# Second mixture of experts: whole experts, tiles of whole weight rows, and another sharing of the low parts between two engines

## The chip, the core and the metric

The kernel runs on one core of one Trainium2 chip. The core has five engines that run side by side and wait for each other through semaphores: PE (TensorE, matrix products, with its weight load PEld), DVE (VectorE), ACT (ScalarE), POOL (GpSimd) and SP (SyncE, which here only issues transfers). Each engine takes its instructions strictly in the order of its own queue. SBUF is the memory beside the engines, PSUM the small memory into which PE accumulates; 16 DMA engines move data between HBM and SBUF.

The metric is the time of the whole program on the device, in microseconds (us). Lower is better.

## The reference, cut to what matters

The program computes two transformer-like blocks one after the other. The change touches only the last stage: the second mixture of experts, in which each of 16 experts picks its own 128 tokens out of 1024.

```python
D_MODEL = 1024; SEQ = 1024; N_EXPERTS_2 = 16; CAPACITY_FACTOR = 2; D_EXPERT_2 = 1024

def expert_choice_ffn(h, w_router, w_gate, w_up, w_down):
    B, S, D = h.shape
    cap = CAPACITY_FACTOR * S // N_EXPERTS_2                      # 128 tokens for each expert
    aff = jax.nn.softmax((h @ w_router).astype(jnp.float32), axis=-1)
    gates, idx = lax.top_k(aff.transpose(0, 2, 1), cap)
    bidx = jnp.arange(B)[:, None, None]
    xe = h[bidx, idx]
    hg = jnp.einsum('becd,edf->becf', xe, w_gate)                 # 128 x 1024 x 1024 per expert
    hu = jnp.einsum('becd,edf->becf', xe, w_up)
    y = jnp.einsum('becf,efd->becd', jax.nn.silu(hg) * hu, w_down)
    y = y * gates[..., None].astype(y.dtype)
    return jnp.zeros_like(h).at[bidx, idx].add(y)

# in second_block: h2 = rmsnorm(x, norm2_w) * (1 + sc2) + sh2;  x = x + gt2 * expert_choice_ffn(h2, ...)
```

All is in float32. The weights of this stage are 16 x 3 matrices of 1024 x 1024, 4 MB each.

## The kernel before

The stage is the class `Moe2`; its `run` (from line 2466) is what the change rewrites, with `load` (line 2335), which issues the weight loads, and the lists made in `open`.

**Three products for one.** PE gets float32 precision out of two parts of each operand. `split_hi_lo` (lines 51 to 61) makes the high part on ACT (a copy that rounds, line 55, tile `wh`) and the low part as the difference of the value and its high part on DVE or, if told so, on POOL (line 61, tile `wl`). `mm3` (lines 64 to 67) then issues three matmuls of 128 x 512: high with high (line 65), high with low (line 66), low with high (line 67). Each reads 128 tokens' activations as the stationary side and 512 columns of weights as the moving side.

**Units and tiles.** An expert is cut in two units of 512 hidden columns (`units`, 32 of them). A unit has six weight tiles of 1 MB, each four blocks of 128 rows by 512 columns: two of gate, two of up, two of down. So a row of a tile is 512 floats out of a matrix row of 1024. The tiles sit in 13 buffers (pools of `WA` = 6 and `WB` = 7), taken in turn; `load(n)` issues the next n transfers on SP's queue in the order of `order`, and a transfer waits until the last reader of its buffer is done.

**Chunks.** `split(u, i)` makes of each product (i = 0 gate, 1 up, 2 down) four chunks of 128 x 1024 floats: one ACT operation for `wh`, one DVE or POOL operation for `wl`; both come from rings of seven buffers (pool `d_s`). A chunk feeds six matmuls, so an expert has 24 chunks and 144 matmuls. POOL makes the low part where `u == 0` (all twelve chunks of the first unit) and for `PL = (1, 0)`: the first two chunks of up, one right behind the other, in each unit, four for an expert. All other low parts are DVE's.

**Order.** The program's order is `gate_up(u)`, then (after an expert's first unit) `gather(e + 1)` and `choose(e + 3)`, then `down(u - 1)`, so that the product of one unit covers the step from `h` to `hh` of the unit before. `gate_up` accumulates in PSUM buffers `pg` and `pu`, `h` is silu(gate) by ACT times up by DVE, one buffer of 512 columns. `down` transposes `h` on PE (tile `tp`), splits it in `hh` and `hl` (one buffer each), and accumulates in `py0` and `py1` over both units of an expert; after the second unit DVE scales the result into `y` (line 2565) and POOL adds it to the output with an indirect DMA (line 2567). `gather` fetches an expert's 128 rows with an indirect DMA of POOL into `xg` (two buffers), scales, transposes and splits them into `xh` and `xl`; `choose` makes the list of rows from one-hot tiles `oh` (DVE, line 2487) and small matmuls (line 2491). A planner that works at build time gives each engine's queue its order from the program's order and modelled times, so neighbouring steps are interleaved on each engine.

Of the kernel before, what the change touches and what calls it, by code (L numbers as in the profile page):

```python
# [9 lines left out]
FR = mybir.dt.float32r  # L10
BF = mybir.dt.bfloat16
# [32 lines left out]
def bcast(ap, shape):  # L44
    return ap.to_broadcast(shape)
# [792 lines left out]
def ind(ap):  # L838
    return bass.IndirectOffsetOnAxis(ap=ap, axis=0)
# [1433 lines left out]

NX = 16
CAP = 128
PL = (1, 0)
XR = D + 1 + NX
WA = 6
WB = 7
# [2 lines left out]
class Moe2:  # L2282
# [3 lines left out]
    def open(self):  # L2286
        k, ident = self.k, self.ident
        nc, tc, T, sb = k.nc, k.tc, k.T, k.sb
        V, PE = nc.vector, nc.tensor
        self.es = ExitStack()  # L2290
        self.ps_s = ExitStack()
        cp = self.cp = self.es.enter_context(tc.tile_pool(name="d_c", bufs=1, reuse_waits="tile"))
        pp = self.pp = self.ps_s.enter_context(
            tc.tile_pool(name="d_rp", bufs=1, space=PSUM, side="right", reuse_waits="tile"))
        self.t_s = ExitStack()
        tp = self.tp = self.t_s.enter_context(tc.tile_pool(name="d_t", bufs=1, side="right", reuse_waits="tile"))
        wr = sb(tp, [P, 8, NX], tag="wr")
# [16 lines left out]
        self.units = [(e, hf) for e in range(NX) for hf in range(2)]  # L2314
        self.order = [(0, i) for i in range(4)]
        for u in range(len(self.units)):
            self.order += [(u + 1, i) for i in range(4) if u + 1 < len(self.units)] + [(u, 4), (u, 5)]
# [18 lines left out]
    def load(self, n):  # L2336
        k = self.k
        for _ in range(n):
            if self.next == len(self.order):
                return  # L2340
            u, i = self.order[self.next]
            e, hf = self.units[u]
# [3 lines left out]
            if i < 4:  # L2346
                src = k.T[("w_gate_2", "w_up_2")[i // 2]][0, e][512 * (i % 2):512 * (i % 2) + 512,
                                                                512 * hf:512 * hf + 512]
            else:
                src = k.T["w_down_2"][0, e][512 * hf:512 * hf + 512, 512 * (i - 4):512 * (i - 4) + 512]  # L2350
            k.nc.sync.dma_start(out=t, in_=src.rearrange("(k p) n -> p k n", p=P))

    def each(self, xc, i, q):
# [112 lines left out]
    def run(self):  # L2466
# [5 lines left out]
        units, wt, load = self.units, self.wt, self.load  # L2472
        slots = WA + WB
        xt, hs, ys = {}, {}, {}
# [6 lines left out]
        with tc.tile_pool(name="d_k", bufs=2, side="right", reuse_waits="tile") as wk, \  # L2481
                tc.tile_pool(name="d_p", bufs=1, space=PSUM, reuse_waits="tile") as pp:

            def choose(e):
                oh = sb(wk, [P, 2, 4, P], BF, tag="oh", bufs=1)
                for h in range(2):
                    V.tensor_tensor(oh[:, h], bcast(self.pos[:, h, :, e:e + 1], [P, 4, P]),
                                    bcast(self.slot.unsqueeze(1), [P, 4, P]), op=OP.is_equal)
                ps = sb(pp, [P, 4, P], tag="tp", bufs=2)[:, 0, 0:2]
                for i in range(NT):  # L2490
                    PE.matmul(ps, oh[:, i // 4, i % 4], self.tk[:, i % 4 * 2 + i // 4], start=i == 0, stop=i == NT - 1)
                V.tensor_scalar(self.idx[:, e:e + 1], ps[:, 0:1], ps[:, 1:2], None, op0=OP.add)

            def gather(e):
                xg = sb(wk, [P, XR], tag="xg")
                dma = G.indirect_dma_start(out=xg, out_offset=None, in_=self.x4_d, in_offset=ind(self.idx[:, e:e + 1]))
                xh = sb(wk, [P, 8, P], FR, tag="xh")
                xl = sb(wk, [P, 8, P], FR, tag="xl")
# [19 lines left out]
                    split_hi_lo(k, xh[:, ks], xl[:, ks], t)  # L2518
                return dma.ins

            def split(u, i):
                r = []
                for c in range(4):
                    wh = sb(wp, [P, 2, 512], FR, tag="wh")
                    wl = sb(wp, [P, 2, 512], FR, tag="wl")
                    src = wt[u, 2 * i + c // 2][:, c % 2 * 2:c % 2 * 2 + 2]
                    split_hi_lo(k, wh, wl, src, lo_eng="pool" if u == 0 or (i, c // 2) == PL else "dve")
                    r.append((wh, wl))
                return r

            def gate_up(u):
                e, hf = units[u]
                xh, xl = xt[e]
                pg = sb(pp, [P, 512], tag="pg", bufs=2)
                pu = sb(pp, [P, 512], tag="pu", bufs=2)
                for i, ps in ((0, pg), (1, pu)):
                    ws = split(u, i)
                    for kk in range(8):
                        wh, wl = ws[kk // 2]
                        mm3(nc, ps, xh[:, kk, :], xl[:, kk, :], wh[:, kk % 2, :], wl[:, kk % 2, :], kk == 0, kk == 7)  # L2540
                h = sb(wk, [P, 512], tag="h", bufs=1)
                A.activation(h, pg, AF.Silu)
                V.tensor_tensor(h, pu, h, op=OP.mult)
                hs[u] = h

            def down(u):
                e, hf = units[u]
                ps = sb(pp, [P, 4, P], tag="tp", bufs=2)
                for j in range(4):
                    PE.transpose(ps[:, j, :], hs[u][:, j * P:(j + 1) * P], ident)  # L2550
                hh = sb(wk, [P, 4, P], FR, tag="hh", bufs=1)
                hl = sb(wk, [P, 4, P], FR, tag="hl", bufs=1)
                split_hi_lo(k, hh, hl, ps)
                if hf == 0:
                    ys[e] = [sb(pp, [P, 512], tag=f"py{n}") for n in range(2)]
                ws = split(u, 2)
                for n in range(2):
                    for j in range(4):
                        wh, wl = ws[2 * n + j // 2]
                        mm3(nc, ys[e][n], hh[:, j, :], hl[:, j, :], wh[:, j % 2, :], wl[:, j % 2, :],  # L2560
                            hf == 0 and j == 0, hf == 1 and j == 3)
                if hf == 1:
                    y = sb(wk, [P, D], tag="y", bufs=1)
                    for n in range(2):
                        V.scalar_tensor_tensor(y[:, 512 * n:512 * n + 512], ys[e][n], self.gcol[:, e:e + 1],
                                               gt2[:, 512 * n:512 * n + 512], op0=OP.mult, op1=OP.mult)
                    G.indirect_dma_start(out=self.out, out_offset=ind(self.idx[:, e:e + 1]), in_=y, in_offset=None,
                                         compute_op=OP.add)
# [6 lines left out]
            for u in range(len(units)):  # L2575
                e, hf = units[u]
                with tc.issue_after(self.exp) if u == 0 else ExitStack():
                    gate_up(u)
                load(4)
                if hf == 0 and e + 1 < NX:  # L2580
                    gather(e + 1)
                    if e + 3 < NX:
                        choose(e + 3)
                if u:
                    down(u - 1)
                    load(2)
            down(len(units) - 1)
        self.es.close()


# [61 lines left out]
```

## Time and profile before

| | |
|---|---|
| median of 3 runs | 3712.46 us (3711.19 to 3718.37) |
| the profiled execution: its time | 3718.16 us |
| the profiled execution: its span, first to last instruction | 3716.4 us |
| busy share of the span | PE 90%, DVE 54%, ACT 35%, POOL 31% |
| mean granted clock of TensorE | 0.959 of full |
| transferred | 856.7 MB, 231 GB/s over the span |

The profile is one execution. An engine's busy time counts its instructions from start to end, and neighbouring ones overlap a little. A wait is put down to what ended it. The stage of the change begins at about 3042 us of the span (routing, with the first low parts beside it), its first large matmul starts at 3083 us, and its last result is added to the output at the end of the span.

### The profile page before, as it was taken

To read this page: it belongs to the slowest core of one execution; us is meant where nothing else is said; L and a number is where in the kernel's file an instruction comes from. 1 tells how busy PE (TensorE), PEld (TensorE's weight loads), DVE (VectorE), ACT (ScalarE), POOL (GpSimd) and SP (SyncE) were. 2 spreads that over 40 slices of the span, in tenths; PEclk is the share of its full clock that TensorE was granted. 3 is DMA by queue.
4 is the path that set the end of the run, shared out by engine and by line. 5 is a ranking of instruction groups with operands and counts; after the bars stand their busy time and mean duration, and the time that the engine had idled before them with its cause. 6 is when DMAs were issued, how large, how long until landed. Compare 5 with 4: busy or idle time off the path is not lost. (4 is left out here: it accounts for less than half of the span.)

```text
span 3716.4 us, 58458 instructions
## 1 busy us (share of the span) xinstructions
PE 3354.9 (90%) x23203; PEld 2589.5 (70%) x23203; DVE 2002.5 (54%) x3563; ACT 1287.1 (35%) x2200; POOL 1164.0 (31%) x1139
## 2 busy tenths in 40 slices
PE   6887899989999999999769988889999977999998
PEld 5676777976676666665368766676777975777776
DVE  7676765252222111211056776735676447999887
ACT  4321132310000000000043333326554236888776
POOL 3477632311001111111122334333232234545343
PEclk9998999999999999999979999999999988999999
DMA  8721224269989999999843234452225556999995
GB/s 239 225 77 52 62 100 153 84 237 383 389 330 398 399 394 397 393 400 408 329 131 99 71 108 117 126 159 86 78 77 141 199 175 248 352 364 366 354 328 191
DMA packets 479317, 856.70 MB, mean 231 GB/s; under 512 B 100779, under 2 KB 294075, under 8 KB 428608
## 3 DMA queue, kind: packets, MB, share of 16 engines
q1 hardware_dynamic: 440288, 786.04, 58.5%
q0 software_dynamic: 16464, 36.39, 4.1%
q10 hardware_dynamic: 22288, 30.48, 2.5%
q8 instruction: 185, 3.03, 0.3%
q14 instruction: 92, 0.75, 0.1%
HBM read 770.37 MB, written 90.74 MB: 232 GB/s over the span
## 5 line engine op out<-in xcount | busy, mean ns | idle before, releaser
L1109 PE MATMUL gu<-w,xt 128*64 128x256 f32 x4096 | 486.4, 385 | 10.5 <-DMA w<-in_expert_w_gate 9.2
L61 DVE TENSOR_TENSOR wl<-w,wh 128x1024 fp32r<-128x1024 f32 x310 | 454.7, 1513 | 45.8 <-ACT wh L55 45.0
L55 ACT ACTIVATE wh<-w 128x1024 fp32r<-128x1024 f32 x412 | 419.7, 1058 | 118.5 <-PE pg L67 32.4
L1109 PEld LDWEIGHTS gu<-w,xt 128*64 128x64 f32 x4096 | 285.2, 137 | 175.5 <-issue 26.1
L1098 POOL DMA_INDIRECT x2d<-ys,si x64 | 114.7, 1792 | 909.8 <-ACT ys L1133 856.2
L61 POOL TENSOR_TENSOR wl<-w,wh 128x1024 fp32r<-128x1024 f32 x102 | 289.3, 2851 | 276.3 <-ACT wh L55 221.2
L1193 PE MATMUL xg<-oh,xh 128*128 128x256 f32 x1024 | 262.1, 293 | 7.1 <-DVE xt L1211 7.1
L1121 ACT ACTIVATE h<-gu 128x256 f32<-128x256 f32 x64 | 24.6, 384 | 673.4 <-PE gu L1109 666.1
L1193 PE MATMUL xg<-oh,xl 128*128 128x256 f32 x1024 | 253.5, 285 | 0.0
L1130 PE MATMUL y<-w,hts 128*64 128x512 f32 x1024 | 235.3, 599 | 1.4 <-ACT ys L1133 1.1
L1193 PEld LDWEIGHTS xg<-oh,xh 128*128 128x128 f32 x1024 | 193.0, 189 | 51.0 <-issue 34.3
L1211 DVE SCALAR_TENSOR_TENSOR xt<-xg,gcolp,row 128x256 f32<-128x256 f32 x128 | 60.3, 481 | 277.2 <-PE xg L1193 216.8
L1193 PEld LDWEIGHTS xg<-oh,xl 128*128 128x128 f32 x1024 | 192.9, 189 | 17.8 <-issue 17.8
L1126 DVE COPY hts<-ht 128x256 f32<-128x256 f32 x64 | 27.1, 424 | 327.9 <-PE y L1130 289.2
L210 PE MATMUL ps<-hth,wh 128*128 128x512 f32 x448 | 180.8, 404 | 2.5 <-DVE qkt L1618 2.5
L212 PE MATMUL ps<-hth,wl 128*128 128x512 f32 x448 | 179.3, 401 | 0.0
L211 PE MATMUL ps<-htl,wh 128*128 128x512 f32 x448 | 178.1, 398 | 0.0
L1130 PEld LDWEIGHTS y<-w,hts 128*64 128x64 f32 x1024 | 72.2, 138 | 121.7 <-issue 108.4
L1122 DVE TENSOR_TENSOR h<-gu,h 128x256 f32<-128x256 f32 x64 | 26.9, 420 | 232.3 <-ACT h L1121 232.3
L65 PE MATMUL ps<-soh,mgh 128*128 128x256 f32 x512 | 149.2, 291 | 0.0
L66 PE MATMUL ps<-sol,mgh 128*128 128x256 f32 x512 | 145.3, 284 | 0.0
L67 PE MATMUL ps<-soh,mgl 128*128 128x256 f32 x512 | 145.0, 283 | 0.0
(947 smaller groups left out, 8490.2 us busy)
## 6 DMA issues: line engine op xcount, KB each, us to landing
w<-in_expert_w_gate SPq DMA_DIRECT2D x128, 1024.0 KB, 9.5
w<-in_expert_w_up SPq DMA_DIRECT2D x128, 1024.0 KB, 10.2
w<-in_expert_w_down SPq DMA_DIRECT2D x128, 1024.0 KB, 10.2
w<-in_w_gate SPq DMA_DIRECT2D x64, 1024.0 KB, 9.1
w<-in_w_up SPq DMA_DIRECT2D x64, 1024.0 KB, 7.4
w<-in_w_down SPq DMA_DIRECT2D x64, 1024.0 KB, 8.7
w<-in_w_in SPq DMA_DIRECT2D x52, 512.0 KB, 4.3
w<-in_w_ada SPq DMA_DIRECT2D x24, 1024.0 KB, 6.5
```

Source lines behind the costliest of these rows:

```text
L55: nc.scalar.activation(hi, src, AF.Copy)
L61: e.tensor_tensor(lo, src, f32(hi), op=OP.subtract)
L65: nc.tensor.matmul(out, lh, rh, start=start, stop=False)
L66: nc.tensor.matmul(out, lh, rl, start=False, stop=False)
L67: nc.tensor.matmul(out, ll, rh, start=False, stop=stop)
L210: k.nc.tensor.matmul(ps, wh[:, kk, j:j + P], rh[:, kk, sl], start=st, stop=False)
L211: k.nc.tensor.matmul(ps, wh[:, kk, j:j + P], rl[:, kk, sl], start=False, stop=False)
L212: k.nc.tensor.matmul(ps, wl[:, kk, j:j + P], rh[:, kk, sl], start=False, stop=sp)
L1098: self.k.nc.gpsimd.indirect_dma_start(out=self.x_d.rearrange("t (o d) -> (t o) d", o=2), out_offset=ind(ix), in_=ys, in_offset=None, compu ...
L1109: PE.matmul(ps[64 * j:64 * j + 64, a, :], xt[:, kk, c0:c0 + 64], ww[:, 256 * j:256 * j + 256], start=kk == 0, stop=kk == 7)
L1130: PE.matmul(py[64 * o:64 * o + 64, :], ht[:, i, 64 * j:64 * j + 64], wd[j][:, i, 512 * o:512 * o + 512], start=j + i == 0, stop=j + i == 2)
L1193: self.k.nc.tensor.matmul(out, x[:, s, kk * P:(kk + 1) * P], oh[:, s, :], start=st, stop=sp)
```

## The change

The stage works by whole experts in place of half experts, with weight tiles of 256 whole rows.

- A tile is now two blocks of 128 rows by all 1024 columns, still 1 MB; an expert has four tiles each of gate (0 to 3), up (4 to 7) and down (8 to 11). A chunk is one block of 128 whole rows, still 128 x 1024 floats, and feeds three matmuls into the first and three into the second 512 columns.
- `gate(e)`, `up(e)` and `down(e)` are steps of their own, each of 8 chunks and 48 matmuls, through one function `product`. The order is gate(e+1), down(e), gather(e+2), choose(e+4), up(e+1), and the loads follow the same order. Gate's two halves take both `pg` buffers, up's both `pu` buffers; `h` holds 1024 columns, `hh` and `hl` a whole expert's; `py0` and `py1` are accumulated within one step.
- POOL makes the low part of one chunk, the first, of tiles 1, 3, 5, 9 and 11 (`PL`): five for an expert, none next to another. For the first expert it also makes all of tiles 0 to 3, 8 and 9 (`P0`): 14 of its 24.
- `choose` has one buffer `oh` of half the size, used twice in a row; `xg` has one buffer.

```diff
-PL = (1, 0)
+PL = ((1, 0), (3, 0), (5, 0), (9, 0), (11, 0))
+P0 = (0, 1, 2, 3, 8, 9)
...
+        G, U, W = range(0, 4), range(4, 8), range(8, 12)
+        self.order = [(0, i) for i in (*G, *U)]
+        for e in range(NX):
+            nx = e + 1 < NX
+            self.order += [(e + 1, i) for i in G if nx] + [(e, i) for i in W] + [(e + 1, i) for i in U if nx]
...
-            t = self.wt[u, i] = k.sb(self.wpools[0 if a else 1], [P, 4, 512], tag="w", bufs=WA if a else WB)
...
+            t = self.wt[e, i] = k.sb(self.wpools[0 if a else 1], [P, 2, D], tag="w", bufs=WA if a else WB)
+            src = k.T[("w_gate_2", "w_up_2", "w_down_2")[i // 4]][0, e][256 * (i % 4):256 * (i % 4) + 256]
...
+                for h in range(2):
+                    oh = sb(wk, [P, 4, P], BF, tag="oh", bufs=1)
+                    V.tensor_tensor(oh, bcast(self.pos[:, h, :, e:e + 1], [P, 4, P]),
...
+                    for i in range(4):
+                        PE.matmul(ps, oh[:, i], self.tk[:, 2 * i + h], start=h + i == 0, stop=h + i == 4)
...
-                    split_hi_lo(k, wh, wl, src, lo_eng="pool" if u == 0 or (i, c // 2) == PL else "dve")
...
+            def product(ps, e, i0, lh, ll):
+                for i in range(i0, i0 + 4):
+                    for c in range(2):
+                        wh = sb(wp, [P, 2, 512], FR, tag="wh")
+                        wl = sb(wp, [P, 2, 512], FR, tag="wl")
+                        pool = (i, c) in PL or (e == 0 and i in P0)
+                        split_hi_lo(k, wh, wl, wt[e, i][:, c].rearrange("p (n f) -> p n f", n=2),
+                                    lo_eng="pool" if pool else "dve")
+                        kk = 2 * (i - i0) + c
+                        for n in range(2):
+                            mm3(nc, ps[n], lh[:, kk], ll[:, kk], wh[:, n], wl[:, n], kk == 0, kk == 7)
...
+            def down(e):
+                hh = sb(wk, [P, 8, P], FR, tag="hh", bufs=1)
+                hl = sb(wk, [P, 8, P], FR, tag="hl", bufs=1)
+                for n in range(2):
+                    ps = sb(pp, [P, 4, P], tag="tp", bufs=2)
                     for j in range(4):
+                        PE.transpose(ps[:, j, :], hs[e][:, n, j * P:(j + 1) * P], ident)
+                    split_hi_lo(k, hh[:, 4 * n:4 * n + 4], hl[:, 4 * n:4 * n + 4], ps)
+                ys = [sb(pp, [P, 512], tag=f"py{n}") for n in range(2)]
+                product(ys, e, 8, hh, hl)
...
+            with tc.issue_after(self.exp):
+                gate(0)
                 load(4)
+                gather(1)
+                choose(3)
+                up(0)
+                load(4)
+            for e in range(NX):
+                if e + 1 < NX:
+                    gate(e + 1)
+                    load(4)
+                down(e)
+                load(4)
+                if e + 2 < NX:
+                    gather(e + 2)
+                    if e + 4 < NX:
+                        choose(e + 4)
+                if e + 1 < NX:
+                    up(e + 1)
+                    load(4)
```

## Rows read from the trace of the kernel before

**Rows 1.** Busy time by stretch: window, length, PE, PEld, DVE, ACT, POOL (x instructions), clock, DMA, GB/s.
```profile
3083.30:3156.20 72.90, 61.36 (x280) 48.69 (x281) 61.20 (x48) 55.32 (x76) 35.40 (x19) 0.89 0.72 257
3156.20:3345.10 188.90, 178.62 (x841) 142.70 (x840) 178.51 (x156) 155.12 (x199) 95.86 (x34) 1.00 1.02 358
```

**Rows 2.** PE's waits, 3083 to the end: total us, times, longest.
```profile
PE pu L66 <- POOL wl L61: 16.2, 18, 2.7
PE pg L66 <- DVE wl L61: 14.1, 15, 2.3
PE pu L66 <- DVE wl L61: 10.1, 1, 10.1
```

**Rows 3.** DVE's results `y`, all and the last pair but one: times, starts.
```profile
L2565 DVE SCALAR_TENSOR_TENSOR y<-py,gcol,gt x32: 732/737/752, 3153.3 to 3707.1; 128x512 f32<-128x512 f32 x32
...
3692.30 1.39 DVE L2565 SCALAR_TENSOR_TENSOR y<-py,gcol,gt 128x512 f32<-128x512 f32 x2
```

**Rows 4.** PE in order of time, steady: start, us, tile and count.
```profile
3307.01 0.39 PE L65 MATMUL pu<-wh,xh 128*128 128x512 f32 x1
3307.24 0.60 PE L2508 MATMUL tp<-ident,xg 128*128 128x128 f32 x4
...
3307.91 0.40 PE L67 MATMUL pu<-wh,xl 128*128 128x512 f32 x1
...
3311.36 0.39 PE L67 MATMUL pu<-wh,xl 128*128 128x512 f32 x1
```

**Rows 5.** DVE in order of time over one expert.
```profile
3307.96 0.74 DVE L2565 SCALAR_TENSOR_TENSOR y<-py,gcol,gt 128x512 f32<-128x512 f32 x1
3308.62 0.68 DVE L61 TENSOR_TENSOR hl<-tp,hh 128x512 fp32r<-128x512 f32 x1
3309.22 4.62 DVE L61 TENSOR_TENSOR wl<-w,wh 128x1024 fp32r<-128x1024 f32 x4
...
3315.49 0.68 DVE L61 TENSOR_TENSOR xl<-xt,xh 128x512 fp32r<-128x512 f32 x1
3316.10 13.59 DVE L61 TENSOR_TENSOR wl<-w,wh 128x1024 fp32r<-128x1024 f32 x8
...
3331.48 1.28 DVE L2487 TENSOR_TENSOR oh<-pos,slot 128x512 bf16<-128x512 f32 x2
...
3345.14 0.74 DVE L2565 SCALAR_TENSOR_TENSOR y<-py,gcol,gt 128x512 f32<-128x512 f32 x1
```

**Rows 6.** POOL in order of time, beside the eight of rows 5.
```profile
3316.76 7.30 POOL L61 TENSOR_TENSOR wl<-w,wh 128x1024 fp32r<-128x1024 f32 x2 [5.17 <-issue]
```

**Rows 7.** Groups by line, 3040 to the end: busy us, mean ns, idle before.
```profile
L61 DVE TENSOR_TENSOR wl<-w,wh 128x1024 fp32r<-128x1024 f32 x310 | 454.7, 1513 | 45.8 <-ACT wh L55 45.0
L61 POOL TENSOR_TENSOR wl<-w,wh 128x1024 fp32r<-128x1024 f32 x74 | 220.7, 3002 | 190.6 <-ACT wh L55 135.4 <-issue 54.8 <-POOL gcol L2500 0.3
```

**Rows 8.** The first units, in order of time: POOL and DVE.
```profile
3048.18 13.88 POOL L61 TENSOR_TENSOR wl<-w,wh 128x1024 fp32r<-128x1024 f32 x6
...
3107.03 9.23 POOL L61 TENSOR_TENSOR wl<-w,wh 128x1024 fp32r<-128x1024 f32 x4
...
3106.68 11.81 DVE L61 TENSOR_TENSOR wl<-w,wh 128x1024 fp32r<-128x1024 f32 x2
```

**Rows 9.** Busy time by stretch, around the long wait (columns as rows 1).
```profile
3112.40:3122.60 10.20, 5.18 (x13) 3.91 (x14) 7.30 (x4) 2.28 (x3) 5.00 (x3) 0.50 0.28 92
```

**Rows 10.** Waits of ACT and DVE, 3083 to the end: total us, times, longest.
```profile
ACT hh L55 <- PE py L66: 18.6, 5, 5.7
...
ACT wh L55 <- DMA w<-in_w_gate: 0.8, 2, 0.4
...
DVE idx L2492 <- PE tp L2491: 6.2, 2, 5.3
```

**Rows 11.** The last unit in order of time: DVE and PE.
```profile
3694.75 0.68 DVE L2543 TENSOR_TENSOR h<-pu,h 128x512 f32<-128x512 f32 x1
...
3700.79 0.50 PE L65 MATMUL py<-wh,hh 128*128 128x512 f32 x1 [0.45 <-ACT hh L55]
```

More of the change, by code (lines that the diff above doesn't have):

```diff
@@ L2340, in load @@
                 return
-            u, i = self.order[self.next]
-            e, hf = self.units[u]
+            e, i = self.order[self.next]
             a = self.next % (WA + WB) < WA
             self.next += 1
-            t = self.wt[u, i] = k.sb(self.wpools[0 if a else 1], [P, 4, 512], tag="w", bufs=WA if a else WB)
[L2346 to L2350, printed above, removed]
+            t = self.wt[e, i] = k.sb(self.wpools[0 if a else 1], [P, 2, D], tag="w", bufs=WA if a else WB)
+            src = k.T[("w_gate_2", "w_up_2", "w_down_2")[i // 4]][0, e][256 * (i % 4):256 * (i % 4) + 256]
             k.nc.sync.dma_start(out=t, in_=src.rearrange("(k p) n -> p k n", p=P))
@@ L2471, in run @@
         wp = self.es.enter_context(tc.tile_pool(name="d_s", bufs=7, reuse_waits="tile"))
-        units, wt, load = self.units, self.wt, self.load
-        slots = WA + WB
-        xt, hs, ys = {}, {}, {}
+        wt, load = self.wt, self.load
+        xt, pgs, hs = {}, {}, {}
         load(WB)
@@ L2484, in choose @@
             def choose(e):
-                oh = sb(wk, [P, 2, 4, P], BF, tag="oh", bufs=1)
+                ps = sb(pp, [P, 4, P], tag="tp", bufs=2)[:, 0, 0:2]
                 for h in range(2):
-                    V.tensor_tensor(oh[:, h], bcast(self.pos[:, h, :, e:e + 1], [P, 4, P]),
+                    oh = sb(wk, [P, 4, P], BF, tag="oh", bufs=1)
+                    V.tensor_tensor(oh, bcast(self.pos[:, h, :, e:e + 1], [P, 4, P]),
                                     bcast(self.slot.unsqueeze(1), [P, 4, P]), op=OP.is_equal)
-                ps = sb(pp, [P, 4, P], tag="tp", bufs=2)[:, 0, 0:2]
-                for i in range(NT):
-                    PE.matmul(ps, oh[:, i // 4, i % 4], self.tk[:, i % 4 * 2 + i // 4], start=i == 0, stop=i == NT - 1)
+                    for i in range(4):
+                        PE.matmul(ps, oh[:, i], self.tk[:, 2 * i + h], start=h + i == 0, stop=h + i == 4)
                 V.tensor_scalar(self.idx[:, e:e + 1], ps[:, 0:1], ps[:, 1:2], None, op0=OP.add)
             def gather(e):
-                xg = sb(wk, [P, XR], tag="xg")
+                xg = sb(wk, [P, XR], tag="xg", bufs=1)
                 dma = G.indirect_dma_start(out=xg, out_offset=None, in_=self.x4_d, in_offset=ind(self.idx[:, e:e + 1]))
@@ L2546, in down @@
[L2546 to L2556, printed above, removed]
-                for n in range(2):
-                    for j in range(4):
[L2559 to L2568, printed above, removed]
@@ new lines, in gate, with up @@
+            def gate(e):
+                pgs[e] = [sb(pp, [P, 512], tag="pg", bufs=2) for _ in range(2)]
+                product(pgs[e], e, 0, *xt[e])
+            def up(e):
+                pu = [sb(pp, [P, 512], tag="pu", bufs=2) for _ in range(2)]
+                h = hs[e] = sb(wk, [P, 2, 512], tag="h", bufs=1)
+                for n in range(2):
+                    A.activation(h[:, n], pgs[e][n], AF.Silu)
+                product(pu, e, 4, *xt[e])
+                for n in range(2):
+                    V.tensor_tensor(h[:, n], pu[n], h[:, n], op=OP.mult)
@@ new lines, in down @@
+            def down(e):
+                hh = sb(wk, [P, 8, P], FR, tag="hh", bufs=1)
+                hl = sb(wk, [P, 8, P], FR, tag="hl", bufs=1)
+                for n in range(2):
+                    ps = sb(pp, [P, 4, P], tag="tp", bufs=2)
+                    for j in range(4):
+                        PE.transpose(ps[:, j, :], hs[e][:, n, j * P:(j + 1) * P], ident)
+                    split_hi_lo(k, hh[:, 4 * n:4 * n + 4], hl[:, 4 * n:4 * n + 4], ps)
+                ys = [sb(pp, [P, 512], tag=f"py{n}") for n in range(2)]
+                product(ys, e, 8, hh, hl)
+                y = sb(wk, [P, D], tag="y", bufs=1)
+                for n in range(2):
+                    V.scalar_tensor_tensor(y[:, 512 * n:512 * n + 512], ys[n], self.gcol[:, e:e + 1],
+                                           gt2[:, 512 * n:512 * n + 512], op0=OP.mult, op1=OP.mult)
+                G.indirect_dma_start(out=self.out, out_offset=ind(self.idx[:, e:e + 1]), in_=y, in_offset=None,
+                                     compute_op=OP.add)
@@ L2574, in run @@
                     choose(e)
[L2575 to L2578, printed above, removed]
+            with tc.issue_after(self.exp):
+                gate(0)
                 load(4)
[L2580 to L2587, printed above, removed]
+                gather(1)
[15 more added lines that the diff above has]
+                    load(4)
         self.es.close()
```

26 lines of the change are left out of this document (removed).

## The prediction

> **What bounds the kernel now.** I read the busy time by stretch first, since only the last 630 us of the span are touched. In the steady part [rows 1] PE is busy 178.6 of 188.9 us and DVE 178.5: two engines at 94%, each fed by the other through rings of seven chunks. PE's waits say which of them holds the other up [rows 2]: PE waits 16.2 us in 18 pieces for low parts of POOL, 14.1 us in 15 pieces for low parts of DVE, and once 10.1 us for one of DVE at the start. All of it is line 66, the first matmul that needs a chunk's low part; the list has hardly anything else. So PE is the engine to keep busy, and low parts that come late are what it lacks.
>
> An expert now takes (3692.30 - 3153.3) / 14 = 38.5 us, from the first y of expert 0 to that of expert 14 [rows 3]; the one in rows 5 takes 3345.14 - 3307.96 = 37.2.
>
> PE's own need: 15 steps of a 512-column matmul between 3307.91 and 3311.36, 0.23 us each; four transposes between 3307.01 and 3307.91 add 0.90 - 2 x 0.23 = 0.44 [rows 4]. An expert has 144 matmuls, 33.1 us, and 16 transposes, 1.8; with its eight small matmuls about 35.2 us. So 3.3 us of 38.5 are not PE's work.
>
> DVE's own need [rows 5]: operations overlap, so the step to the next start counts, 0.08 less than the duration: y 0.66, hl 0.60 (h, of the same size, the same), xl 0.61, oh 0.60, and four low parts 4.54, or 1.135 each. An expert has 20 low parts, 22.7 us, two each of y, hl, h, xl and oh, 6.1, and one idx, 0.1: 28.9 us. But it was busy nearly all of 37. The rest is POOL: eight low parts that have two of POOL beside them take 13.59 us where 4.62 + 4 x 1.135 = 9.16 would do, so **each low part on POOL costs DVE 2.2 us** [rows 5, 6], twice what DVE saves by not making it. Over the stage a DVE low part has a mean of 1.513 us against 4.62 - 3 x 1.135 = 1.21 alone: 310 x 0.30 = 94 us lost to 74 of POOL, of which seven ran before x was there [rows 7, 8], so 94 / 67 = 1.4 us each on average, less than 2.2 because DVE sometimes had nothing to do or read PSUM meanwhile.
>
> The Trainium skill, in "SBUF — State Buffer", section "Who interferes with whom", explains this: a VectorE instruction with two SBUF inputs takes its second through the read port that GpSimd also uses, and one blocks the other for a whole instruction; the trace agrees, with 2.2 us for low parts, and with y, which reads PSUM and in 32 times never took over 0.752 [rows 3]. By that rule taken strictly every part of POOL costs the whole 2.2, which is the first rival below; by the measured mean it costs 1.4, which is the forecast.
>
> **The change, part by part.** *Matmuls, transposes, high parts:* 144, 16 and 24 for an expert before and after, the same shapes; nothing.
>
> *Whole weight rows.* The same 192 loads of 1 MB, with rows twice as long. They could only help where someone waits for weights: ACT waited 0.8 us for gate's and about as much for down's, in all [rows 10]. I take 0; bounds -2 and, should a load come late in the new order, +2.
>
> *One more part on POOL.* DVE then makes 19: 28.9 - 1.1 = 27.8 us of its own. With five of POOL at the mean of 1.4 us it needs 34.8 (now 28.9 + 5.6 = 34.5); at the full 2.2 it needs 38.8 (now 37.7).
>
> *Spread out.* In each pair DVE loses 4.4 us and POOL needs 7.3 for two chunks which PE eats in 12 x 0.23 = 2.8 [rows 4 to 6]; a single one costs half of that between chunks that DVE makes at 1.135, faster than PE's 1.4. The 16.2 us for POOL's parts [rows 2] should therefore mostly go. Next late is DVE itself, which has the same load as now.
>
> *Whole experts.* The steps gate, down, up are twice as long and so half as many, and hh is no longer overwritten behind the product before it: that wait holds ACT 18.6 us in five pieces [rows 10], with the high parts of later chunks queued behind it, for which DVE and POOL wait, and then PE.
>
> For both parts together I take PE's waits outside the start, 30.3 us [rows 2], from about 2.0 us an expert to 1.1: **-14 us**. Bounds: 0.2 left, 15 x 1.8 = -27; and DVE at 38.8 with 0.9 idle, 39.7 an expert, 15 x 1.2 = +18. I sit nearer to the first, since the mean of 1.4 is measured over 67 parts and the full 2.2 only where DVE had no gap.
>
> *The start.* Now four parts of POOL run in a row (9.23 us), one DVE part between them takes most of 11.8 us, and PE stands still for 10.1 [rows 2, 8]; behind it 13 instructions run at a granted clock of 0.50, the lower of the two levels, after PE had stood still [rows 9], 13 x 0.23 or up to 3 us more. After the change seven parts of gate(0) again fall beside the routing, but the four in a row move to down(0), tiles 8 and 9, behind all of gate(1). A full ring is 7 x 6 x 0.23 = 9.7 us of PE work, about the 9.2 that POOL needs; the ring will hardly be full so early, as up(0) is now seven parts for DVE, with xl and oh of three experts. I leave 5 us of the 13: **-8**; bounds -13 and +3.
>
> *The end.* Now the last unit's h is made while PE works on the down before [rows 11]; afterwards nothing lies behind up(15) but down(15). PE waits for the h step 0.6, transposes 0.8, hh 0.6 and hl 0.6, or 2.6, against some 0.6 now: **+2**. Bounds: 0, and the 6.0 us from h to the first py of now.
>
> *One buffer for oh and for xg.* The second oh waits on DVE for four small matmuls, with low parts queued behind it and PE behind those. The nearest row is idx, which waited for such matmuls 6.2 us in 2 pieces out of 16 [rows 10]. In 13 of 16 calls: 0 to +6; I take 0, since DVE runs behind PE's wishes, not ahead. xg is refilled an expert ahead; 0.
>
> Sum: 0 - 14 - 8 + 2 + 0 = -20 us. The profiled execution, 3718.2 us with 1.8 around its span, would come to 3698; it lies 5.7 above the median of the runs shown, and the start's and POOL's waits are no accident of that one, so I put the sum on the median: 3712.5 - 20 = **3692.5 us**.
>
> **The rivals.** *DVE becomes the bound by the fifth part: slower.* If DVE has no gap, each of POOL's five parts costs the full 2.2 us, and DVE needs 27.8 + 11.0 = 38.8 us an expert, above PE's 35.2 and above today's 38.5. It decides from (38.5 - 27.8) / 5 = 2.1 us a part. With 0.9 us of idle time that is +18, the start gives only -4, the end costs 2: 3728. For it: DVE's 94% in the steady part and the 13.59 us. Against it: the mean of 1.4, and y, h, hl, which read PSUM. 23%. The Trainium skill warns of it in "Perfetto Trace Analysis", section "Optimizing Scalar/DVE Operations": as GpSimd and VectorE share a read port, moving work between these two might not help. The rows bear that out for a busy DVE, 2.2 us against 1.1.
>
> *PE becomes the bound.* Single parts fit between DVE's and PE waits 0.2 us an expert: -27, start -12, end +1, so 3674. For it: DVE's need at the mean, 34.8, is below PE's 35.2. Against it: two engines at the same load seldom mesh without loss. 22%.
>
> *It doesn't do what it says.* The planner decides the queues; POOL's parts may stand late or side by side again behind the indirect DMAs in its queue, and the fifth eats what the longer steps give: steady 0, start -4, end +2, so 3710. 15%.
>
> **How the numbers follow.** Forecast 40%, 3682 to 3704; PE-bound 22%, 3662 to 3682; no gain 15%, 3705 to 3719; DVE-bound 23%, 3720 to 3738. The forecast and PE-bound are faster by over 0.2% (7.4 us, about what a measurement of this kernel can tell): with a small part of the forecast's upper end taken off, 60%; same 17%; slower 23%. The range leaves out a tenth at either end: 3664 to 3731. The likeliest case alone: 3682 to 3704.
>
> **What would show it.** Right: PE's wait for POOL's parts falls from 16.2 to a few us; the y operations stand 36.5 to 38 us apart; no wait near 10 us at the start; ACT's wait of hh for py is gone; the mean of a DVE low part stays near 1.5. Wrong: that mean rises to 1.7 or more with DVE busy throughout (the fifth part), or y stays 38.5 apart with waits moved to DVE's parts; a new wait of about 9 us within down(0); oh waiting for small matmuls; ACT waiting for weights.

## The result, and the profile after

The changed kernel is slower: 3762.24 us (median, 3759.08 to 3765.78) against 3715.41 for the kernel before on the same chip, a ratio of 1.0125 with an interval of 1.0106 to 1.0144. The forecast was 3692.5, its range 3664 to 3731. The profiled execution has a span of 3764.0 us against 3716.4.

First the results `y` (times, first and last start):

```profile
L2554 DVE SCALAR_TENSOR_TENSOR y<-py,gcol,gt x32: 731/740/751, 3143.7 to 3754.5; 128x512 f32<-128x512 f32 x32
```

Beside the same row of before [rows 3], the first `y` comes 9.6 us earlier, and from the first to the last it takes 610.8 us in place of 553.8. So the start gave what was forecast (8 us), and the steady part with the end lost 57. The groups of the low parts by line (busy us, mean ns, idle before):

```profile
L61 DVE TENSOR_TENSOR wl<-w,wh 128x1024 fp32r<-128x1024 f32 x295 | 452.0, 1571 | 73.4 <-ACT wh L55 72.9
L61 POOL TENSOR_TENSOR wl<-w,wh 128x1024 fp32r<-128x1024 f32 x89 | 238.8, 2688 | 291.1 <-ACT wh L55 198.6 <-issue 65.8 <-DVE oh L2484 15.9
```

DVE makes 15 low parts fewer than in [rows 7] and is busy with them just as long, 452.0 us against 454.7. PE's waits from 3083 us to the end (total us, times, longest):

```profile
PE py L67 <- DVE hl L61: 28.4, 8, 4.2
PE py L65 <- ACT hh L55: 6.9, 9, 1.1
PE tp L2487 <- DVE oh L2484: 5.9, 3, 4.3
PE pg L67 <- DVE xl L61: 5.4, 4, 2.2
PE pg L66 <- DVE wl L61: 5.3, 3, 4.2
PE tp L2548 <- DVE h L2540: 3.8, 2, 2.3
```

POOL's parts, 16.2 us in [rows 2], are gone from the list, as forecast, and so is the wait of 10.1. In their place stands one that the prediction didn't have: the first matmul of down that needs `hl`. Three engines in order of time at one such place (start, us, tile, count, idle before); DVE:

```profile
3246.04 11.30 DVE L61 TENSOR_TENSOR wl<-w,wh 128x1024 fp32r<-128x1024 f32 x6
3257.26 1.28 DVE L61 TENSOR_TENSOR hl<-tp,hh 128x512 fp32r<-128x512 f32 x2
3260.34 1.22 DVE L61 TENSOR_TENSOR wl<-w,wh 128x1024 fp32r<-128x1024 f32 x1 [1.80 <-ACT wh L55]
```

POOL:

```profile
3248.06 2.61 POOL L61 TENSOR_TENSOR wl<-w,wh 128x1024 fp32r<-128x1024 f32 x1 [2.63 <-ACT wh L55]
3252.69 2.43 POOL L61 TENSOR_TENSOR wl<-w,wh 128x1024 fp32r<-128x1024 f32 x1 [2.02 <-ACT wh L55]
```

PE:

```profile
3251.30 1.03 PE L2548 MATMUL tp<-ident,h 128*128 128x128 f32 x8
3253.09 0.50 PE L65 MATMUL py<-wh,hh 128*128 128x512 f32 x1 [0.76 <-ACT hh L55]
...
3253.89 0.39 PE L66 MATMUL py<-wl,hh 128*128 128x512 f32 x1
3257.99 1.22 PE L67 MATMUL py<-wh,hl 128*128 128x512 f32 x2 [3.71 <-DVE hl L61]
3259.01 0.63 PE L65 MATMUL py<-wh,hh 128*128 128x512 f32 x1
...
3263.70 0.50 PE L67 MATMUL py<-wh,hl 128*128 128x512 f32 x1
```

PE's queue has the transposes of `h` behind the last matmul of gate, so nothing covers the way from `h` to `hl` but the few matmuls of down that don't need `hl`; and in DVE's queue `hl` stands behind six low parts, which two of POOL stretch from 6 x 1.135 + 0.08 = 6.9 us to 11.3. The windows of this place (columns as rows 1) show the second loss:

```profile
3251.20:3257.80 6.60, 2.32 (x14) 1.47 (x12) 6.60 (x5) 3.04 (x6) 2.43 (x1) 0.95 0.90 316
3257.90:3265.00 7.10, 7.01 (x19) 5.53 (x20) 3.08 (x4) 2.81 (x3) 0.00 (x0) 0.58 0.85 306
```

After PE has stood still, matmuls are 0.43 us apart in place of 0.23 (11 steps from 3259.01 to 3263.70), until the granted clock, 0.58 on average in the second window, comes back. Meanwhile the ring of seven chunks is full, ACT waits for PE, and DVE, which was late a moment before, has nothing to do:

```profile
3259.25 1.06 ACT L55 ACTIVATE wh<-w 128x1024 fp32r<-128x1024 f32 x1 [4.75 <-PE py L67]
```

To compare kernels I count two things from 3078 us on: *pauses*, the steps between starts of PE's instructions that are over 0.6 us, less 0.23 each; and *lower clock*, the steps of 0.38 to 0.50 us of large matmuls, less 0.23 each.

| kernel | median us | pauses us | lower clock us |
|---|---|---|---|
| before | 3715.4 | 51.6 | 4.7 |
| after | 3762.2 | 68.9 | 25.1 |
| e1_turn_early | 3738.4 | 58.7 | 13.7 |
| e2_no_pool | 3696.2 | 23.7 | 8.9 |
| e5_before_no_pool | 3672.7 | 12.3 | 2.4 |
| e6_four_parts | 3738.2 | 53.7 | 20.6 |
| e13_port_read | 3731.9 | 49.0 | 13.1 |
| e17_two_buffers | 3671.5 | 13.2 | 2.9 |
| e20_two_buffers_five | 3756.2 | 77.2 | 16.0 |

The counts are taken from the profiled executions. Of the 47.6 us by which the span grew, pauses are 17.3 and the lower clock 20.4; the other 10 I have not divided.

### The profile page after: what moved, and what is told of

Its sections match the earlier page's. It is cut to its first block, busy times and chain, and to the rows that moved or that the text cites. A ratio compares the mean times of both kernels' runs of the same rounds, so it can differ in the third digit from the quotient of the medians.

```text
span 3764.0 us, 58498 instructions
## 1 busy us (share of the span) xinstructions
PE 3378.0 (90%) x23203; PEld 2609.7 (69%) x23203; DVE 2020.2 (54%) x3548; ACT 1297.4 (34%) x2200; POOL 1160.9 (31%) x1154
## 5 line engine op out<-in xcount | busy, mean ns | idle before, releaser
L61 DVE TENSOR_TENSOR wl<-w,wh 128x1024 fp32r<-128x1024 f32 x295 | 452.0, 1571 | 73.4 <-ACT wh L55 72.9
L55 ACT ACTIVATE wh<-w 128x1024 fp32r<-128x1024 f32 x412 | 428.7, 1062 | 174.0 <-PE py L67 67.0
L61 POOL TENSOR_TENSOR wl<-w,wh 128x1024 fp32r<-128x1024 f32 x117 | 307.3, 2630 | 375.8 <-ACT wh L55 283.4
```

What stands on the lines that cost most here:

```text
L55: nc.scalar.activation(hi, src, AF.Copy)
L61: e.tensor_tensor(lo, src, f32(hi), op=OP.subtract)
```

## The experiments

Kernels that were timed together share the runs of before, whose median lay between 3712.6 and 3715.6. "Parts" are POOL's low parts outside the first expert's own list.

### What POOL's parts cost

e2_no_pool, the changed kernel with

```diff
-PL = ((1, 0), (3, 0), (5, 0), (9, 0), (11, 0))
+PL = ()
```

> Edit: the changed kernel with no low parts on POOL after the first expert's (PL empty, P0 as it is); DVE makes 24 an expert. Rival B (port): each of POOL's parts blocks DVE 1.7 us or more and saves it 1.135, so without them DVE needs 29 + 4.5 = 33.5 us an expert, below PE's 35.2, and the time falls below the kernel before, 3690 to 3710. Theory A (late step from h to hl): hl still stands behind six low parts of down in DVE's queue; these take 6 x 1.135 = 6.8 us in place of 11.3, with one or two more in front, so hl comes 2 to 3 us earlier and PE's pause of 5 us shrinks to 2 or 3: 3715 to 3740.

3696.23 us, ratio 0.9951 (0.9934 to 0.9968): 66 us less by taking POOL's help away. e12_one_part keeps `((5, 0),)` alone:

> Edit: the changed kernel with one of POOL's parts for an expert (the first chunk of tile 5) in place of five. No part: 3696; four: 3738; five: 3762. If a part costs alike wherever DVE stands: 3696 + 10, so 3704 to 3710. If a part is free as long as DVE with its block stays below PE's 35.2 us (33.5 - 1.1 + 2.2 = 34.6): 3693 to 3700, and the cost begins with the second or third.

3694.39 (0.9932 to 0.9965): the first part is free. e6_four_parts leaves out `(11, 0)`:

> Edit: the changed kernel with four of POOL's parts, the first chunk of tile 11 given back to DVE. Five parts against none are 66 us. If each part costs alike: 3762 - 13, so 3745 to 3753. If the fifth tips DVE over PE's rate, as my rival had it (decides from 38.5 us an expert): most of the 47 us come back, 3710 to 3725. If what matters is what stands ahead of hl in DVE's queue (tile 11's part is one of two there, 2.2 us each): the pause of 5 us falls to 3 and the clock is lost less often: 3725 to 3740.

3738.24 (1.0042 to 1.0076): four cost 42, the fifth 24 more. The part left out also stood ahead of `hl`, so number and place change together here. PE's wait for `hl`, 28.4 us in 8 pieces with five parts, is now

```profile
PE py L67 <- DVE hl L61: 27.9, 12, 3.2
```

The single wait is shorter, as the third expectation had it, but there are more and the total is the same; whether number or place saves the 24 us, no run tells. The kernel before, without its pairs, is e5_before_no_pool:

```diff
-lo_eng="pool" if u == 0 or (i, c // 2) == PL else "dve"
+lo_eng="pool" if u == 0 else "dve"
```

> Edit: the kernel before with no low parts on POOL after the first unit's twelve. It asks whether POOL's parts were already a loss there, and so whether the whole experts bring anything. Port theory: each part costs DVE 1.5 us and saves it 1.135, PE then waits little and an expert falls from 38.5 us towards 36: 15 x 2 to 2.5, so 3675 to 3690, about as fast as the whole experts without POOL's parts (3696). Rival: the gain of those came from the whole experts, and here DVE alone is too slow or nothing changes: 3705 to 3725.

3672.73, ratio 0.9877 (0.9861 to 0.9894): the four paired parts that the tuned kernel always had cost it 43 us. The group of DVE's low parts:

```profile
L61 DVE TENSOR_TENSOR wl<-w,wh 128x1024 fp32r<-128x1024 f32 x372 | 437.3, 1228 | 25.2 <-ACT wh L55 24.8 <-PE pu L67 0.2
```

It makes 62 more than in [rows 7] in 17 us less, at 1.23 us each and not 1.51. In e4_before_apart POOL's four chunks of before stand apart (`PL = ((0, 2), (1, 1))`, test `(i, c) in PL`):

> Edit: the kernel before, with POOL's four low parts of an expert apart: the third chunk of gate and the second of up in each unit, in place of the first two of up. One part of the change alone. My prediction's step 'spread out': PE's waits for POOL's parts (16.2 us) mostly go and the time falls by 8 to 16 us, 3698 to 3707. Rival: a part of POOL costs DVE the same 1.4 to 2.2 us wherever it stands, and the wait only changes its name: 3708 to 3722.

3722.18, 1.0021 (1.0011 to 1.0032): spreading them out gains nothing.

### Is it the reading

e13_port_read and e14_port_write are e2_no_pool with work on POOL that spares DVE nothing, at the start of up, into the buffer of `y` of that expert:

```diff
+                y = yt[e] = sb(wk, [P, D], tag="y", bufs=1)
+                for _ in range(2):
+                    G.tensor_tensor(y, gt2, gt2, op=OP.subtract)   # e13
+                for _ in range(4):
+                    G.memset(y, 0.0)                               # e14
```

> Edit: the changed kernel without POOL's parts, with two subtractions of 128 x 1024 floats on POOL for each expert that read an unused pair of SBUF inputs and write the tile y before its time; nobody waits for them. It measures POOL's hold on DVE by itself. If a POOL operation that reads SBUF blocks DVE's low parts for its whole length: DVE operations with two SBUF inputs beside it take 2.2 us longer, 33.5 + 4.4 = 37.9 us an expert, above PE's 35.2: 3696 + 15 x 2 to 2.7, so 3725 to 3740. If only the late parts on POOL were the trouble (PE waiting for them): 3692 to 3700.

> Edit: as the run with two subtractions on POOL, but with four memsets of 128 x 1024 floats in their place, which read nothing. If the hold comes from reading: no DVE operation is lengthened and the time is 3692 to 3700. If any POOL operation holds DVE up: 1 us or more for each memset, 3705 to 3740.

e13: 3731.88 (1.0028 to 1.0061), 36 us over e2, with 32 subtractions that keep POOL busy for 78 us. e14: 3697.47 (0.9935 to 0.9968), 1 us over it. POOL's two subtractions in e13 in order of time, and DVE beside them:

```profile
3445.84 4.75 POOL L2540 TENSOR_TENSOR y<-gt 128x1024 f32<-128x1024 f32 x2
```

```profile
3445.78 3.06 DVE L61 TENSOR_TENSOR wl<-w,wh 128x1024 fp32r<-128x1024 f32 x1
3448.76 0.21 DVE L2488 TENSOR_SCALAR idx<-tp 128x1 int32<-128x1 f32 x1
3448.89 2.24 DVE L2484 TENSOR_TENSOR oh<-pos,slot 128x512 bf16<-128x512 f32 x1
3451.06 1.22 DVE L61 TENSOR_TENSOR wl<-w,wh 128x1024 fp32r<-128x1024 f32 x1
```

A low part takes 3.06 us in place of 1.22, an `oh` 2.24 in place of 0.68; as soon as POOL is done they are short again. The groups of e14:

```profile
L61 DVE TENSOR_TENSOR wl<-w,wh 128x1024 fp32r<-128x1024 f32 x372 | 447.3, 1238 | 39.6 <-ACT wh L55 29.4
...
L2540 POOL MEMSET y<- 128x1024 f32 x64 | 61.2, 957 | 58.3 <-DMA out<-y,idx 55.7
```

61 us of POOL that only writes leave DVE's mean at 1.238, where e2 has 1.240. So it is POOL's reading that holds up DVE. The Trainium skill states just this in "SBUF — State Buffer", section "Who interferes with whom": two SBUF inputs on VectorE contend with a GpSimd instruction that reads SBUF, and not with one that only writes it; both runs agree.

### The pause ahead of down

e1_turn_early moves transposes and split of `h` into the middle of the next gate:

```diff
+                product(pgs[e], e, 0, *xt[e], range(2))
+                if e:
+                    turn(e - 1)
+                product(pgs[e], e, 0, *xt[e], range(2, 4))
```

> Edit: the changed kernel, with h's transposes and split put into the middle of the next expert's gate (after its tiles 0 and 1) in place of its end; nothing else. Theory A (late step from h to hl): in the changed kernel PE meets h's eight transposes only behind the last gate matmul, then waits about 1 us for hh and 4 us for hl, and after that 5 us pause the clock is granted at 0.50 for 3.4 to 6.8 us, once for each expert. With the transposes 24 matmuls earlier the waits py<-hl (28.4 us in 8) and py<-hh (6.9 us) go, with most of the matmuls at the lower clock (about 25 us): 3762 - 35 - 20, so 3700 to 3715. Rival B (port): DVE is the bound by POOL's fifth part, so PE waits for low parts of the weights instead and the time stays at 3745 to 3765.

3738.43 (1.0046 to 1.0084), 24 us less, which lies between the two expectations. PE's waits, the first four:

```profile
PE tp L2553 <- DVE h L2543: 9.9, 5, 2.2
PE tp L2487 <- DVE oh L2484: 9.8, 6, 3.7
PE pg L66 <- DVE wl L61: 7.9, 6, 2.2
PE pg L67 <- DVE xl L61: 7.6, 5, 3.0
```

The wait for `hl` is all but gone (0.6 us), and the four longest that are left are all for DVE. With both edits, e3_turn_early_no_pool:

> Edit: both edits at once: h's transposes in the middle of gate and no low parts on POOL after the first expert's. If A and B are separate causes the gains add up: 3670 to 3690, with the y operations about 36 us apart. If A alone is the cause, the same as with the transposes moved alone, within 8 us. If DVE without POOL's help is too slow for PE, slower than with the transposes moved alone, by up to 20 us.

3695.1 (0.994 to 0.9972), the same as e2_no_pool's 3696.2. So the pause is no cause of its own: without POOL's parts it isn't there to be moved away. With them it costs 24 us. And e1 and e3 differ by POOL's five parts alone, with the pause out of the way: that is 43 us, the larger share of the 66.

### The rewritten order

Without parts the changed kernel takes 3696.2 and the kernel before 3672.7. Where do these 23.5 us come from? e8_half_rows is e2_no_pool with each load in two transfers of half rows:

```diff
+            for n in range(2):
+                src = rows[:, 512 * n:512 * n + 512]
+                k.nc.sync.dma_start(out=t[:, :, 512 * n:512 * n + 512], in_=src.rearrange("(k p) n -> p k n", p=P))
```

> Edit: the changed kernel without POOL's parts, each 1 MB tile loaded in two transfers of half rows (512 floats, as before the change) in place of one of whole rows. If the longer rows matter: slower by 5 us or more than 3696. If, as predicted, nobody waits for weights: 3692 to 3700, with only the times to landing longer.

3700.91 (3697.15 to 3705.3) beside 3692.43 to 3698.34 for e2: half rows, with twice as many transfers, cost about 5 us, and the two ranges overlap a little. e10_gather_first_early is e3 with gather(e+2) and choose(e+4) ahead of down(e):

> Edit: the changed kernel without POOL's parts, with h's transposes in the middle of gate, and with gather(e+2) and choose(e+4) ahead of down(e) in place of behind it. In the runs without POOL's parts the first eight experts take 35 us each with no wait of PE, the last eight 38 to 42, where the gather's transposes and the small matmuls of choose stand at the end of up, one waiting for the other. If that is what is left, experts 9 to 12 fall to 35 or 36: 3680 to 3690. If it is not the place, 3692 to 3700.

3689.23 (0.9914 to 0.9947), 6 less than e3. e15_before_small gives e5_before_no_pool the change's buffers: `oh` of half the size used twice, one `xg`.

> Edit: the kernel before without POOL's parts (3673), with the change's smaller buffers: oh of half the size used twice, xg single. Whole experts without POOL's parts are 23 us slower than half experts without them, and PE's waits there are for the small matmuls of choose, oh and the gather's chain. If the small buffers are the cause: 3685 to 3697. If it is the longer steps, which leave PE's queue no other product to put between: 3670 to 3677.

3696.85 (0.9934 to 0.9967), 24 more than e5, the very size that was sought. But half of it lies at the start: its first `y` comes at 3149.5 us, e5's at 3136.9 and e2's at 3135.0. So the equal sums prove little. To make room for two buffers each, e16_one_tile_less gives up one of 13 weight tiles (`WB = 6`); it is the base of e17_two_buffers:

```diff
-WB = 7
+WB = 6
-oh = sb(wk, [P, 4, P], BF, tag="oh", bufs=1)
+oh = sb(wk, [P, 4, P], BF, tag="oh", bufs=2)
-xg = sb(wk, [P, XR], tag="xg", bufs=1)
+xg = sb(wk, [P, XR], tag="xg", bufs=2)
```

> Whole experts without POOL's parts (e2_no_pool, 3696.2 us), with 12 weight tiles in place of 13. It is the base for e17_two_buffers, for which the tile makes room. ACT waited little for weights there, so every theory expects the time of e2_no_pool: 3692 to 3702. Well above it would mean that the ring of weights is tight.

> e16_one_tile_less with two buffers each for oh and for xg. Theory A (the two single buffers are what the rewritten order lost against the kernel before without POOL's parts, 3696.2 against 3672.7): 15 to 24 us below e16_one_tile_less, 3672 to 3685, and PE's waits for oh (5.8 us) and the one for idx gone. Rival B (the steps of whole experts lose it: the transposes of xg, the small matmuls and the transposes of h stand together between up and gate whatever the buffers): within 6 us of e16_one_tile_less, and PE still waits for xt and h there.

e16: 3684.18 (0.9902 to 0.9946), 12 less than e2, against every expectation. e17: 3671.51, ratio 0.989 (0.9868 to 0.9911), 12.7 less than e16 and level with e5. PE in order of time, e2_no_pool first, at the step from up to gate:

```profile
3432.39 1.04 PE L2504 MATMUL tp<-ident,xg 128*128 128x128 f32 x8
...
3434.58 0.24 PE L2487 MATMUL tp<-tkb,oh 128*128 128x2 bf16 x4 [1.16 <-ACT xt L2508]
3436.21 0.27 PE L2487 MATMUL tp<-tkb,oh 128*128 128x2 bf16 x4 [1.39 <-DVE oh L2484]
3437.47 1.12 PE L2548 MATMUL tp<-ident,h 128*128 128x128 f32 x4 [1.00 <-DVE idx L2488]
```

and e17_two_buffers, the same three steps:

```profile
3427.86 1.03 PE L2548 MATMUL tp<-ident,h 128*128 128x128 f32 x8
...
3432.87 1.04 PE L2504 MATMUL tp<-ident,xg 128*128 128x128 f32 x8
...
3437.89 0.35 PE L2487 MATMUL tp<-tkb,oh 128*128 128x2 bf16 x8
```

With one `oh`, the second four small matmuls wait for DVE in the middle of PE's queue; with two, all eight go at once. The two kernels differ by a weight tile and by the order of PE's queue as well: e16, with one `oh`, has matmuls of up between the two fours and waits there for 0.71 us at most. e18_before_one_xg and e19_before_one_oh take e15's two edits one by one:

> The kernel before without POOL's parts (e5_before_no_pool, 3672.7 us), with one buffer for xg. Of the 24 us that one xg and a half-size oh used twice cost together there (e15_before_small, 3696.9), xg's share is asked. If xg: 3690 or more. If oh: 3672 to 3678.

> The kernel before without POOL's parts, with the half-size oh used twice and two buffers for xg. If oh carries the 24 us: 3690 or more. If xg does: 3672 to 3678. Should neither this nor e18_before_one_xg be near 3697, the two add up, or the order that is planned anew for each kernel makes the difference.

3689.64 (+17 on e5) and 3704.17 (+31), while both together cost 24: the sizes don't add. e21_before_one_tile_less is e5 with `WB = 6`:

> The kernel before without POOL's parts (3672.7 us) with 12 weight tiles in place of 13. In the rewritten kernel one tile less took 12 us away (3696.2 to 3684.2). If a smaller ring helps by itself, 3658 to 3668. If it only changed the order that is planned around the single buffers of oh and xg, which this kernel doesn't have so small: 3668 to 3678.

3680.99 (3675.77 to 3686.45), 8 more than e5 and outside both expectations. So a smaller ring is no gain of its own; what differs in e16's trace is the order of PE's queue, with the small matmuls inside up. One tile less moved the two kernels by -12 and +8, though ACT waited for weights only 1.1 us in e16 and not at all in e21. So a change of this size can come with the queues being planned anew, and the 12.7, 17 and 31 us above are no clean prices of a buffer.

### The parts on a kernel without the other loss

e20_two_buffers_five is e17_two_buffers with the change's five parts:

> e17_two_buffers (3671.5 us: whole experts, two buffers for oh and for xg, 12 tiles, no parts on POOL outside the first expert) with the change's five parts on POOL. If the parts cost by themselves what they cost in the changed kernel (3762.2 - 3696.2 = 66), 3728 to 3746. If a good part of the 66 came from the single buffers that POOL's parts made late, 3690 to 3720. If the port costs the full 2.2 us for each of 80 parts less 1.1 saved and PE has no slack, 3671.5 + 88 = 3760 at most.

3756.22, 1.0106 (1.0084 to 1.0128): 85 us more than e17 for 77 parts (POOL makes 89 in its trace and 12 in e17's), or 1.10 each. That this is 2.2 less 1.135 is partly luck: by the table above 64 of the 85 are pauses and 13 the lower clock, and among the pauses are waits for POOL's own parts, which the changed kernel didn't have, 28.9 us in all:

```profile
PE pu L66 <- POOL wl L61: 10.8, 3, 4.3
PE py L66 <- POOL wl L61: 10.7, 11, 1.7
...
PE pg L66 <- POOL wl L61: 7.4, 3, 5.5
```

What a part does to DVE is seen on single instructions:

```profile
3238.32 2.77 DVE L2484 TENSOR_TENSOR oh<-pos,slot 128x512 bf16<-128x512 f32 x1
3241.02 0.68 DVE L61 TENSOR_TENSOR xl<-xt,xh 128x512 fp32r<-128x512 f32 x1
...
3286.11 0.68 DVE L2540 TENSOR_TENSOR h<-pu,h 128x512 f32<-128x512 f32 x1
3286.71 3.42 DVE L61 TENSOR_TENSOR wl<-w,wh 128x1024 fp32r<-128x1024 f32 x1
```

while POOL has

```profile
3237.96 2.58 POOL L61 TENSOR_TENSOR wl<-w,wh 128x1024 fp32r<-128x1024 f32 x1 [2.83 <-ACT wh L55]
...
3286.63 2.42 POOL L61 TENSOR_TENSOR wl<-w,wh 128x1024 fp32r<-128x1024 f32 x1 [0.17 <-issue]
```

`oh` takes 2.09 us longer than its 0.68, the low part 2.20 longer than its 1.22. In e2_no_pool the same five cost 66. The next section's table shows the difference mostly from expert 5 on, where e2 takes 39.0 us an expert already without parts and e17 36.1.

## Why the prediction was wrong

**The sum that came about.** From before, 3715.6: its four parts away, -43 (e5); the order and the single buffers, +23.5 (e2); five parts, +66 (after). Together +47. The shares depend on the order in which the edits are taken. By way of e17 and e20 they are -43 (e5), then -1 for whole experts with two buffers and a tile less (e17), +85 for five parts (e20), and +6 for the single buffers and the 13th tile (after): once POOL's parts are in place, the buffers show as 6 us, no more than a new order of the queues can do.

**One more part, spread out, whole experts: -14 forecast.** The step that failed is the choice between 1.4 and 2.2 us as the price of a part, and the yardstick beside it. As a mean hold on DVE the 1.4 was about right: in the changed kernel 295 low parts are longer by 1.571 - 1.21, 106 us for the 82 parts of POOL that ran after the first seven, or 1.3 each, and 1.6 with the 23 us by which `xl` and `oh`, which the prediction left out, are longer than in e2. But the mean is lower where DVE stands idle, and idle time doesn't make a part cheaper for a kernel in which DVE is short elsewhere. The kernel paid 66 us for 77 parts, which is 2.0 each when the saved 1.135 is counted back. The yardstick was today's 38.5 us an expert, which held POOL's loss already. The numbers for the right question stood in the prediction: DVE's own 28.9 plus four low parts at 1.135 is 33.4, below PE's 35.2. In the first experts DVE needed no help, as e2 shows, with PE busy all 189.0 us from 3156 to 3345. The same stretch of e2, of e1 and of the changed kernel (columns as rows 1):

```profile
3156.00:3345.00 189.00, 189.00 (x897) 153.60 (x897) 182.49 (x188) 166.19 (x212) 21.02 (x15) 1.00 1.03 395
...
3156.00:3345.00 189.00, 178.46 (x822) 142.06 (x821) 182.81 (x147) 151.56 (x196) 101.11 (x39) 0.97 0.97 353
...
3156.00:3345.00 189.00, 165.79 (x736) 131.98 (x735) 164.83 (x135) 138.60 (x174) 80.07 (x35) 0.94 0.93 330
```

With n parts at the full 2.2 DVE needs 33.4 + 1.07 n, an estimate from [rows 5]: 34.5 for one, 37.7 for four, 38.8 for five. Beside it stands what an expert took, in us, from the first `y` of expert 0 to that of expert 5, and from there to that of expert 14:

| kernel | parts | larger of DVE's sum and PE's 35.2 | experts 0 to 5 | experts 5 to 14 |
|---|---|---|---|---|
| e5_before_no_pool | 0 | 35.2 | 35.2 | 37.7 |
| before | 4 | 37.7 | 37.5 | 39.1 |
| e3_turn_early_no_pool | 0 | 35.2 | 34.9 | 38.7 |
| e1_turn_early | 5 | 38.8 | 38.5 | 40.9 |
| e2_no_pool | 0 | 35.2 | 34.9 | 39.0 |
| e12_one_part | 1 | 35.2 | 35.7 | 38.5 |
| e6_four_parts | 4 | 37.7 | 41.1 | 40.5 |
| after | 5 | 38.8 | 42.2 | 42.2 |
| e17_two_buffers | 0 | 35.2 | 35.1 | 36.1 |
| e20_two_buffers_five | 5 | 38.8 | 43.2 | 40.6 |

In the first experts the sum fits where there is no pause ahead of down (before, e1): there DVE's need sets the pace, in e1 with DVE busy 182.8 of 189.0 us and PE 178.5. With the pause (e6, after, e20) an expert takes 3.4 to 4.4 us more than the sum, and in the changed kernel DVE (164.8 us) and PE (165.8) stand still in turn. From expert 5 on even the kernels without parts are slower than PE's need, for reasons that are only in part known, and the parts cost less there. So it is partly luck that the sum over 15 experts, 38 us for four parts and 54 for five, comes near the measured 42 or 43 and 66 or 85. Two kernels don't fit in the first experts: e4 with 40.1 in place of 37.7, and e13 with 36.1, where 33.4 and two holds of 2.2 make 37.8.

**Spread out** was worth nothing. The wait for POOL's parts went in the changed kernel, but it is back in e20 with the same five parts, 28.9 us, and in e4, where 5.9 of it are left, the time is no better. DVE was the short engine, so in the changed kernel and in e4 PE waited under other names. That sentence, "next late is DVE itself, which has the same load as now", stood there, and the -14 ignored it.

**Whole experts.** ACT's wait of `hh` for `py` [rows 10] did go. But the prediction had a term for the way from `h` to `hl` only at the end and so put it at nothing in the steady part, without a reason; the queues have the transposes behind gate and `hl` behind six low parts. e1 puts that at 24 us. In themselves the longer steps are worth nothing: e17 and e5 are level.

**One buffer for oh and for xg: 0 forecast, bound +6.** Mis-sized, by how much stays open: 12.7 us between e16 and e17, 17 to 31 in the kernel before, but 6 at most with POOL's parts in place (e20 and after), and none of these is free of the order that is planned anew. The bound came from `idx` waiting in two calls of 16 [rows 10], the wrong row: there both halves of `oh` are made in one go [rows 5], and no small matmul waits between them. What was left out is PE: with one buffer its queue can stand still in the middle of a step, with everything behind it, 5.9 us for `oh` in the changed kernel. In e19's trace PE never waits for `oh`, so what makes that kernel slower stays open.

**Whole weight rows: 0.** Right within its bounds or nearly, if e8's 5 us are not all due to the doubled number of transfers; ACT waited 3.1 us for weights in the changed kernel, 1.6 in the one before.

**The start: -8.** Right: the first `y` came 9.6 us earlier. **The end: +2.** About +4 in waits: PE waited twice for `h` in the last step, 3.8 us, and 0.7 for `hh`, in place of 0.6.

**The rivals.** The DVE-bound one, 3728 with 23%, had the mechanism. It fell short as it counted against today's 38.5, and as it had neither the pause ahead of down nor the buffers nor the lower clock. The mean of a low part rose to 1.57, between the 1.5 that was to show the forecast right and the 1.7 that was to show it wrong: it is diluted by those parts that met no POOL, and so no good mark.

**Versions that beat both.** e17_two_buffers (3671.5) and e5_before_no_pool (3672.7, one line of before) are 1.1 to 1.2% faster than the kernel before.

## What to carry to other kernels

Before moving more work to a helping engine, work out what the busy engine would need with no help at all, and set that, not today's interval, beside the other bound. A price per helper that is measured as a mean over stretches with idle time is too low; take it where the helped engine has no gap, and look for what the busy engine needs next behind the held instructions, since a hold there comes on top. A buffer halved in the middle of an engine's strict queue is priced by what stands behind the wait in that queue, not by how often some neighbour waited.

## What the runs showed of the hardware

- One subtraction of POOL over 128 x 1024 floats held a DVE instruction with two SBUF inputs for 1.6 to 2.2 us in the places shown (e13, e20), `oh` as well as a low part, while 64 memsets of the same size left DVE's mean where it was (e14). Where an indirect DMA of POOL ran just ahead of the subtraction, a low part of the changed kernel took 4.42 us (at 3737.36), 3.2 more than alone.
- A pause of PE was paid for again behind it: in the place shown 11 steps of 0.43 us followed, at the lower of the two levels (1.2 and 2.4 GHz), 2.2 us more than at 0.23; over the stage of the changed kernel 25.1 us beside 68.9 us of pauses.
